# A one-layer hybrid decoder step: weight loads and stores moved from SP's DMA queue to POOL's, and a changed table of planned delays for TensorE's order

## Chip, core and metric

The kernel runs on one core of one Trainium2 chip. The metric is the device time of one execution in microseconds; lower is better. The time before is 1907.03 us, the median of three runs (1903.8, 1907.03 and 1909.56). The core has five engines that run their own instruction streams: PE (TensorE; its weight loads are listed as PEld), DVE (VectorE), ACT (ScalarE), POOL (GpSimd) and SP (SyncE, which here only issues DMAs).

## What is computed

One layer for a prompt of 1024 tokens and 8 samples of 8 tokens, 1088 columns in all, width 1024, float32:

```python
h = rmsnorm(x, norm_g)
p = jnp.einsum('btd,dc->btc', h, w_in)
q, k, v, ga, ps, gb, ma, mb = _split(p, IN_SIZES)
o = swa_banded(q, k, v, rel_bias, sinks_g)                # branch A, window 128
ya = jnp.einsum('btc,cd->btd', o * jax.nn.silu(ga), w_out_a)
yb_raw, wkv_T = rwkv_time_mix(ps, shift0, wkv0, ...)      # branch B, 16 heads of 64
yb = jnp.einsum('btc,cd->btd', yb_raw * jax.nn.silu(gb), w_out_b)
merged = jax.nn.sigmoid(ma) * ya + jax.nn.sigmoid(mb) * yb
out = x + jnp.einsum('btd,de->bte', merged, w_o)          # then a final rmsnorm
```

Inside `rwkv_time_mix` the projections r, k, v are mixed with those of the token before (z = ps + (prev - ps) * mu), decay and rate come from low-rank products, and a recurrence over the tokens updates one 64 x 64 state a head; its result is normalised by head and, with the term r*k*v added, multiplied by the gate. The outputs are y, the last keys and values, the states, and the last shift row.

## The kernel before

**Dense products.** All matrices are cut into 93 weight tiles of 1024 x 128. A float32 product is made of three float32r products: the weight is split in a high part `whi` (ACT, line 170) and a rest `wlo` (line 171), and the activations likewise in `hhi` and `hlo`. `load_w` (line 163) issues the load of a tile into the single buffer `wraw` and the two operations of the split. Each tile is multiplied with three chunks of columns (364, 364 and 360), 24 products a chunk, in two PSUM banks called d. The rest of the weight is computed on POOL in the recurrence's stage and on DVE in attention (`dve_lo`, line 276). A weight's buffers are double, so the rest of one tile waits until PE has finished the tile two before.

**Stages.** `start` normalises x. `rwkv` (line 484) runs the recurrence on 16 pieces s: four pairs of head groups times four quarters of 256 tokens. `attention` runs the window attention with the projections of its queries, and `final` the last projections. In `rwkv` one piece passes through these steps:

- front (lines 556 and 597, `quarter` once for each of two groups): loads zk, zr and zv of what `project` stored, the low-rank products (lo), the norm of the keys (kn), the product bo on the bonus term (line 686), the products A of the 64-token chunks, and two transposes t_k and t_v.
- invert (line 764): the 32 x 32 triangular blocks go to DRAM and come back in another layout (TM and TR), 31 steps of two operations follow on DVE (lines 784 and 786), and the result goes through DRAM again.
- merge (line 791): loads the inverse into `ti` (line 807) and joins the halves by the products q_a and q_b.
- chain (line 829): four chunks of 64 tokens in sequence. Each has three dependent products in bank c (lines 857, 864 and 869), with copies by ACT and DVE between them (xs and vsu), and ends with line 877, which adds the decayed state `sp` that POOL computed at line 853.
- posts (line 542): the products gc and gv of the head norm, three POOL operations (lines 945, 951 and 952), and the store to `d_y` (line 953). samples (line 532): the same recurrence for the samples, with products ss.

`project` (line 419) makes r, k and v: the evacuation in `shift_tile` writes two scaled copies by ACT (lines 403 and 404), POOL adds the shifted one (lines 405 and 412) into a buffer `zz`, of which there are two that other evacuations share, and line 424 stores it to `d_z`.

**What sets the order.** PE's order in these stages is written by a planner, `drive` (line 142). Each step is a generator that yields the delay after which its next product may stand, counted on the planner's clock, which advances with the products placed. A step that is ready is placed; otherwise four products of the dense stream are. The delays are the constants of lines 35 and 41: WI between the end of a front and the merge, WB between kn and bo, WM before q_a, WH and WS between the steps of a chain, WP between those of a post, WA, WD and WT elsewhere. HOLD is the time for which a single PSUM bank is kept free after its last use. The orders of ACT, DVE, POOL and SP are made by a scheduler from priorities. Each engine executes its list in order; so does SP's DMA queue, so that a DMA that waits holds up all that stand behind it.

Of the kernel before, what the change touches and what calls it, by code (L numbers as in the profile page):

```python
# [16 lines left out]
KT = 8  # L17
# [14 lines left out]
QORD = (4, 5, 6, 7) + tuple(range(NQS, 4)) + tuple(range(NQS))  # L32
FILL = (0, 0, 0, 0, 2, 2, 3, 2)
QD = 4
HOLD = 1.4
WV = 13.0
NYS = 6
MAN = {mybir.EngineType.PE, mybir.EngineType.SP, mybir.EngineType.Pool}
WX = 0.06
YPR = (200000, 0, 0)  # L40
WI, WD, WB, WA, WM, WH, WS, WP, WT = 34.0, 3.5, 9.0, 0.8, 4.0, 1.0, 1.7, 4.0, 10.0


T_LORA = 0
# [37 lines left out]
class Prog:  # L82
# [33 lines left out]
    def step(self, st):  # L116
# [7 lines left out]
        for tag in self.used:  # L124
            self.free[tag] = self.clk + HOLD
        self.used = set()
# [36 lines left out]
    def load_w(self, idx, pool=None, bufs=2, tag="", rpool=None, rbufs=1):  # L163
        nc = self.nc
        pool = pool or self.wp
        raw = (rpool or self.wp).tile([P, KT, P], F32, tag="wraw", name=f"wraw{idx}", bufs=rbufs)
        hi = pool.tile([P, KT, P], F32R, tag="whi" + tag, name=f"whi{idx}", bufs=bufs)
        lo = pool.tile([P, KT, P], F32R, tag="wlo" + tag, name=f"wlo{idx}", bufs=bufs)
        nc.sync.dma_start(raw, self.I["w"][idx].rearrange("p (k c) -> p k c", k=KT))
        nc.scalar.activation(hi, raw, AF.Copy)  # L170
        (nc.vector if self.dve_lo else nc.gpsimd).tensor_tensor(lo, raw, hi.bitcast(F32), ALU.subtract)  # L171
        return hi, lo
# [246 lines left out]
    def project(self, g):  # L419
        nc, ep = self.nc, self.ep  # L420
        base = T_RKVG + 4 * g
        for j in range(3):
            def out(c0, c1, z):
                nc.sync.dma_start(self.d_z[g][j][:, c0:c1], z[:, :c1 - c0])
                if j == 2:
                    self.mark(f"z{g}_{c0}")
            yield from self.shift_tile(base + j, 8 * j + g, out)
# [501 lines left out]
    def post(self, g, nm, t, w, y):  # L929
        nc, cp = self.nc, self.pp  # L930
        y = y[:, :w]
        rs = cp.tile([P, 320], F32, tag="gb", name=f"gn{nm}", bufs=2)[:, :w]
        parts = self.split(cp, y, w, f"c{nm}")
        yield None, WP, "t"
        ps = self.ps("t", f"gc{nm}")[:, :w]
        self.sum2(ps, self.cen, parts)
        nc.scalar.activation(rs, ps, AF.Square)
        nc.vector.tensor_copy(y, ps)
        parts = self.split(cp, rs, w, f"v{nm}")
        yield None, 1.0 + WP, "t"  # L940
        p2 = self.ps("t", f"gv{nm}")[:, :w]
        self.sum2(p2, self.bone, parts)
        nc.scalar.activation(rs, p2, AF.Ln, scale=1.0 / HD, bias=self.cst(C_EPS + 1, 1))
        nc.scalar.activation(rs, rs, AF.Exp, scale=-0.5)
        nc.gpsimd.tensor_tensor(y, y, rs, ALU.mult)
        nc.scalar.activation(y, y, AF.Identity, scale=self.par(Q_LG + g), bias=self.par(Q_LB + g))
        bt = cp.tile([P, 320], F32, tag="gb", name=f"bt{nm}", bufs=2)[:, :w]
        gt = cp.tile([P, 320], F32, tag="gb", name=f"gt{nm}", bufs=2)[:, :w]
        nc.sync.dma_start(bt, self.d_b[g][:, t:t + w])
        nc.sync.dma_start(gt, self.d_g[g][:, t:t + w])  # L950
        nc.gpsimd.tensor_tensor(y, y, bt, ALU.add)
        nc.gpsimd.tensor_tensor(y, y, gt, ALU.mult)
        nc.sync.dma_start(self.d_y[g][:, t:t + w], y)


    def attention(self, hs):
# [550 lines left out]
```

## Time and profile before

| | |
|---|---|
| median of three runs | 1907.03 us |
| the profiled execution's own time | 1908.33 us |
| its span, first to last instruction | 1906.5 us |
| PE busy | 1677.5 us (88%), mean granted clock 0.94 |
| DVE busy | 1193.9 us (63%) |
| ACT busy | 969.7 us (51%) |
| POOL busy | 414.6 us (22%), 490 instructions |
| moved by DMA | 209.33 MB, mean 110 GB/s |

Busy time is time in which an engine executes; a DMA's issue is not counted in it. The granted clock is the share of full speed that TensorE ran at. A wait is listed with the engine and line that waited, the one that released it, the total, the count and the longest.

### The profile page before, as it was taken

The page shows a single profiled execution, that of the slowest core. Times are in us where ns is not written, and L with a number is a line of the kernel's source. Part 1 is how long each engine was busy: PE and PEld are TensorE (multiplying, and loading weights), DVE is VectorE, ACT ScalarE, POOL GpSimd, SP SyncE. Part 2 cuts the span into 40 slices and gives each one's busy share as a digit, 9 for nine tenths or more (in the row PEclk, how much of TensorE's full clock was granted, in tenths as well). Part 3 has the DMA queues.
Part 4 walks back from the last instruction along what each step waited for, and adds up shares of the span by engine and source line. Part 5 has one row for each costly group of instructions (what it writes and reads, how often), then busy time and mean ns, then how long its engine had stood idle before and what let it go on. Part 6 is the DMA issues. An engine that isn't in the chain of part 4 may idle for free.

```text
span 1906.5 us, 33558 instructions
## 1 busy us (share of the span) xinstructions
PE 1677.5 (88%) x11744; PEld 1580.2 (83%) x11744; DVE 1193.9 (63%) x3563; ACT 969.7 (51%) x2494; POOL 414.6 (22%) x490
## 2 busy tenths in 40 slices
PE   5899697887787897786999887899999999999998
PEld 4899686776786887786889887889999889899997
DVE  6324868878768748669743778652266677544543
ACT  5346545654464545455545646644456765422232
POOL 4443223322422332123225112233100010000000
PEclk9999898988988988898999998999999999999999
DMA  4333423433333233332324333324422254374531
GB/s 161 134 97 113 108 85 86 120 92 96 107 84 102 79 101 113 103 86 88 99 72 138 113 105 98 93 75 138 146 91 65 75 167 131 103 247 139 174 110 58
DMA packets 217645, 209.33 MB, mean 110 GB/s; under 512 B 108452, under 2 KB 193044, under 8 KB 217444
## 3 DMA queue, kind: packets, MB, share of 16 engines
q1 hardware_dynamic: 216900, 204.22, 35.4%
q0 software_dynamic: 576, 2.96, 0.5%
q8 instruction: 93, 1.52, 0.3%
q14 instruction: 76, 0.62, 0.1%
HBM read 144.01 MB, written 65.07 MB: 110 GB/s over the span
## 4 chain that ended last, share of the span: by engine, by line
PE 58%; DVE 23%; ACT 6%; issue 5%; DMA 4%; POOL 2%; SPq 1%; DVEq 0%; POOLq 0%; ACTq 0%
PE d L110 37%; PE wo L110 5%; DVE TR L786 4%; DVE Tt L784 4%; PE c L110 3%; DVE KB L678 2%; PE s L110 2%; PE y L110 2%; PE o L110 2%; DVE vsu L877 1%; PE A L110 1%; PE pt L108 1%; POOL wlo L171 1%; DMA xt<-in_x 1%; DVE sg L650 1%
## 5 line engine op out<-in xcount | busy, mean ns | idle before, releaser
L110 PE MATMUL d<-hhi,whi 128*128 128x364 f32 (+1 forms) x1656 | 588.2, 355 | 52.9 <-ACT sho L414 23.0
L110 PE MATMUL d<-hlo,whi 128*128 128x364 f32 (+1 forms) x1656 | 567.1, 342 | 7.9 <-DVE hlo L350 6.9
L110 PEld LDWEIGHTS d<-hhi,whi 128*128 128x128 f32 x1656 | 331.1, 200 | 63.3 <-ACT sho L414 24.8
L110 PEld LDWEIGHTS d<-hlo,whi 128*128 128x128 f32 x1656 | 330.5, 200 | 13.3 <-DVE hlo L350 9.6
L110 PE MATMUL d<-hhi,wlo 128*128 128x364 f32 (+1 forms) x1656 | 336.9, 341 | 0.0
L110 PEld LDWEIGHTS d<-hhi,wlo 128*128 128x128 f32 x1656 | 285.5, 195 | 3.5 <-issue 3.3
L171 POOL TENSOR_TENSOR wlo<-wraw,whi 128x1024 fp32r<-128x1024 f32 x56 | 134.1, 2394 | 269.6 <-PE d L110 119.2
L786 DVE TENSOR_TENSOR TR<-TR,Tt 96x90 f32<-96x90 f32 (+26 forms) x496 | 142.7, 288 | 11.4
L784 DVE TENSOR_TENSOR Tt<-TM,TR 96x90 f32<-96x90 f32 (+26 forms) x496 | 138.8, 280 | 11.5
L170 ACT ACTIVATE whi<-wraw 128x1024 fp32r<-128x1024 f32 x90 | 95.0, 1056 | 73.0 <-PE d L110 52.7
L405 POOL TENSOR_TENSOR zz<-zz,pad 128x364 f32<-128x364 f32 (+1 forms) x75 | 74.1, 989 | 185.1 <-ACT zz L404 122.8
L853 POOL TENSOR_TENSOR sp<-vsu,pc 64x128 f32<-64x128 f32 x128 | 58.3, 455 | 222.4 <-DVE vsu L877 211.6
L877 DVE SCALAR_TENSOR_TENSOR vsu<-c,pc,sp 64x64 f32<-64x64 f32 x240 | 68.0, 283 | 18.9 <-PE c L110 14.3
L1080 ACT ACTIVATE sc<-sc,st 128x256 f32<-128x256 f32 (+1 forms) x128 | 61.8, 484 | 34.1 <-DVE st L1076 34.1
L403 ACT ACTIVATE pad<-d,prm 128x364 f32<-128x364 f32 (+1 forms) x75 | 40.7, 543 | 72.9 <-PE d L110 62.0
L1341 POOL TENSOR_TENSOR xr<-xr,frs 128x256 f32<-128x256 f32 x2 | 1.8, 934 | 341.5 <-ACT frs L1338 341.5
L678 DVE TENSOR_TENSOR KB<-e,sg 64x256 f32<-64x256 f32 x128 | 67.5, 537 | 1.2
L110 PE MATMUL d<-yhi,whi 128*128 128x364 f32 (+1 forms) x192 | 65.2, 340 | 0.0
L110 PE MATMUL d<-ylo,whi 128*128 128x364 f32 (+1 forms) x192 | 63.9, 333 | 0.0
L110 PE MATMUL d<-oh,whi 128*128 128x364 f32 (+1 forms) x192 | 63.2, 329 | 0.0
L110 PE MATMUL d<-ol,whi 128*128 128x364 f32 (+1 forms) x192 | 62.9, 328 | 0.0
L110 PE MATMUL wo<-ml,whi 128*128 128x416 f32 (+1 forms) x192 | 60.5, 329 | 0.0
(331 smaller groups left out, 3578.0 us busy)
## 6 DMA issues: line engine op xcount, KB each, us to landing
wraw<-in_w SPq DMA_DIRECT2D x93, 512.0 KB
d_z<-zz SPq DMA_DIRECT2D x48, 182.0 KB
zv<-d_z SPq DMA_DIRECT2D x48, 128.0 KB
d_m<-sp SPq DMA_DIRECT2D x32, 182.0 KB
TM<-s SPq DMA_DIRECT2D x72, 64.0 KB
stageo<-d_o SPq DMA_DIRECT2D x8, 544.0 KB
d_z<-zz SPq DMA_DIRECT2D x24, 180.0 KB
w<-in_lora SPq DMA_DIRECT2D x32, 128.0 KB
```

The lines of the kernel that those rows point to most:

```text
L108: self.nc.tensor.transpose(out, lhsT, rhs)
L110: self.nc.tensor.matmul(out, lhsT=lhsT, rhs=rhs, **kw)
L170: nc.scalar.activation(hi, raw, AF.Copy)
L171: (nc.vector if self.dve_lo else nc.gpsimd).tensor_tensor(lo, raw, hi.bitcast(F32), ALU.subtract)
L403: nc.scalar.activation(pad[:, 1:1 + m], ps[:, :m], AF.Copy, scale=mu)
L405: nc.gpsimd.tensor_tensor(z[:, :m], z[:, :m], pad[:, 0:m], ALU.add)
L678: nc.vector.tensor_tensor(KB[hr, :4, j, :], v64(t)[hr], d64(Pi, 1)[hr], ALU.mult)
L784: nc.vector.tensor_tensor(tv, M[s // 16][:np_, s % 16:s % 16 + 1, s + 1:32].to_broadcast([np_, cc, w]), R[:np_, 0:cc, s:s + 1].to_broadcas ...
L786: nc.vector.tensor_tensor(R[:np_, 0:cc, s + 1:32], R[:np_, 0:cc, s + 1:32], tv, ALU.add)
L853: nc.gpsimd.tensor_tensor(sp[h], vsu[h, c, :, h], pc[h, c].unsqueeze(2).to_broadcast([64, 2, HD]), ALU.mult)
L877: nc.vector.scalar_tensor_tensor(dst, pn[h, i, h], pc[h, c, i:i + 1], sp[h, i], ALU.mult, ALU.add)
L1080: nc.scalar.activation(sc[k], sc[k], AF.Exp, bias=st[:, 0, k:k + 1], accum_out=st[:, 1, k:k + 1])
```

## The change

The constants of the planner change, and three DMA statements name POOL's queue in place of SP's: the weight loads where POOL computes the rest (56 of the 90 that `load_w` issues; in attention and after they stay on SP), the 72 stores of z, and the 32 stores of y.

```diff
-HOLD = 1.4
+HOLD = 2.0
...
-WI, WD, WB, WA, WM, WH, WS, WP, WT = 34.0, 3.5, 9.0, 0.8, 4.0, 1.0, 1.7, 4.0, 10.0
+WI, WD, WB, WA, WM, WH, WS, WP, WT = 38.0, 3.5, 15.0, 0.8, 5.0, 1.4, 2.4, 5.0, 10.0
...
-        nc.sync.dma_start(raw, self.I["w"][idx].rearrange("p (k c) -> p k c", k=KT))
+        (nc.sync if self.dve_lo else nc.gpsimd).dma_start(raw, self.I["w"][idx].rearrange("p (k c) -> p k c", k=KT))
...
-                nc.sync.dma_start(self.d_z[g][j][:, c0:c1], z[:, :c1 - c0])
+                nc.gpsimd.dma_start(self.d_z[g][j][:, c0:c1], z[:, :c1 - c0])
...
-        nc.sync.dma_start(self.d_y[g][:, t:t + w], y)
+        nc.gpsimd.dma_start(self.d_y[g][:, t:t + w], y)
```

**PE, the first front's bo.** Before, the product bo0_0 of group 0, quarter 0 stands inside the third chunk of tile 5 (`d5_2`):

```order
L110 MATMUL d5_2_1197<-hhi728_153,whi5_956 128x360
L110 MATMUL d5_2_1197<-hlo728_154,whi5_956 128x360
L110 MATMUL bo0_0_1210<-shib0_0_1134,bone_171 128x256
L110 MATMUL bo0_0_1210<-slob0_0_1135,bone_171 128x256
L110 MATMUL A0_000_1227<-RA0_0_1125,KB0_0_1126 128x128
L110 MATMUL A0_001_1228<-RA0_0_1125,KB0_0_1126 128x128
```

Now it stands behind the whole first chunk of tile 6 (`d6_0`):

```order
L110 MATMUL d6_0_1240<-hhi0_143,whi6_1084 128x364
L110 MATMUL d6_0_1240<-hlo0_144,whi6_1084 128x364
L110 MATMUL d6_0_1240<-hhi0_143,wlo6_1085 128x364 x8
L110 MATMUL bo0_0_1272<-shib0_0_1134,bone_171 128x256
L110 MATMUL bo0_0_1272<-slob0_0_1135,bone_171 128x256
L110 MATMUL A0_000_1289<-RA0_0_1125,KB0_0_1126 128x128
L110 MATMUL A0_001_1290<-RA0_0_1125,KB0_0_1126 128x128
```

The last 12 products of d5_2 and the 24 of d6_0 have moved ahead of bo.

**PE, the third chunk of the last chain.** Before, products of a dense tile (`d37`) stand between the three steps of chunk c3_32 (the products y are its outputs):

```order
L110 MATMUL c3_32_14366<-vsu6_3_13244,am6_3_13246 128x128
L110 MATMUL c3_32_14366<-vsu6_3_13244,am7_3_13537 128x128
L110 MATMUL y3_32_14369<-r02_730,vsu6_3_13244 128x128
L110 MATMUL y3_32_14369<-r03_731,vsu6_3_13244 128x128
L110 MATMUL d37_0_14349<-hhi0_143,whi37_14085 128x364
L110 MATMUL d37_0_14349<-hlo0_144,whi37_14085 128x364
L110 MATMUL d37_0_14349<-hhi0_143,whi37_14085 128x364
L110 MATMUL d37_0_14349<-hlo0_144,whi37_14085 128x364
L110 MATMUL d37_0_14349<-hhi0_143,wlo37_14086 128x364 x4
L110 MATMUL c3_32_14366<-xs3_32_14367,ti_726 128x64 x2
L110 MATMUL d37_0_14349<-hhi0_143,wlo37_14086 128x364 x4
```

Now the steps follow each other, with no dense product between:

```order
L110 MATMUL c3_32_14916<-vsu6_3_13850,am6_3_13852 128x128
L110 MATMUL c3_32_14916<-vsu6_3_13850,am7_3_14255 128x128
L110 MATMUL y3_32_14919<-r02_730,vsu6_3_13850 128x128
L110 MATMUL y3_32_14919<-r03_731,vsu6_3_13850 128x128
L110 MATMUL c3_32_14916<-xs3_32_14917,ti_726 128x64 x2
L110 MATMUL c3_32_14916<-vsu6_3_13850,kbt6_3_13853 128x128
L110 MATMUL c3_32_14916<-vsu6_3_13850,kbt7_3_14256 128x128
L110 MATMUL y3_32_14919<-am6_3_13852,vsu6_3_13850 128x128
L110 MATMUL y3_32_14919<-am7_3_14255,vsu6_3_13850 128x128
```

The dense tiles that stood here and behind, down to tile 42, now stand earlier.

**SP and POOL, the merge of piece 9 (pair 2, quarter 1).** Before, SP's queue has weight loads (`wraw`) and stores of merge gates (`d_m`) around the store of the inverse (line 788) and its load into `ti` (line 807):

```order
L455 DMA d_m1_136<-sp56_0_8874 128x364
L1260 DMA mb1_0_17425<-d_m1_136 128x364
L455 DMA d_m1_136<-sp56_364_8928 128x364
L788 DMA s22_1_8539<-TR2_1_8542 352x1x32 x3
L169 DMA wraw27_9548<-in_w 128x1024
L455 DMA d_m1_136<-sp56_728_8981 128x360
L807 DMA ti_726<-s22_1_8539 32x8x32 x4
L779 DMA TR2_2_9373<-in_ri 96x352
```

Now at the same place:

```order
L589 DMA zk_5_3_10393<-d_z5_1_99 128x320
L788 DMA s22_1_9300<-TR2_1_9303 352x1x32 x3
L586 DMA w2_5_3_10389<-in_lora 128x256
L807 DMA ti_726<-s22_1_9300 32x8x32 x4
L950 DMA gt4_0_9854<-d_g4_111 128x256
L779 DMA TR2_2_10050<-in_ri 96x352
```

The load of tile 27, which stood between lines 788 and 807, has left the queue. On POOL it now follows the computation of the rest of tile 26, which frees the buffer, and each store of z (`d_z`) follows its addition:

```order
L853 TENSOR_TENSOR sp1_30_8419<-vsu2_3_7102,pc2_3_7103 64x128 x2
L171 TENSOR_TENSOR wlo26_7878<-wraw26_7876,whi26_7877 128x1024
L169 DMA wraw27_8069<-in_w 128x1024
L405 TENSOR_TENSOR zz6_0_7913<-zz6_0_7913,pad6_0_7912 128x364
L424 DMA d_z6_0_101<-zz6_0_7913 128x364
L405 TENSOR_TENSOR zz6_364_7954<-zz6_364_7954,pad6_364_7953 128x364
L424 DMA d_z6_0_101<-zz6_364_7954 128x364
L171 TENSOR_TENSOR wlo27_8071<-wraw27_8069,whi27_8070 128x1024
L945 TENSOR_TENSOR ysb1_20_7375<-ysb1_20_7375,gn2_2_7887 128x256
```

Nothing was taken off POOL for these rows; SP's list is shorter by 160 DMAs and POOL's longer by as many.

## The prediction

> **What bounds the kernel now.** I read the busy times by stage first, because one share over the whole span hides that this program has stages with different limits. Columns: stretch, its length, busy time of PE, PEld, DVE, ACT and POOL (with counts), granted TensorE clock, DMA share, GB/s.
>
> ```profile
> 61.30:177.50 116.20, 106.32 (x633) 104.55 (x634) 28.10 (x79) 51.85 (x126) 46.87 (x58) 0.96 0.38 127
> 177.50:1322.00 1144.50, 959.45 (x7057) 897.36 (x7056) 807.31 (x2522) 614.93 (x1647) 318.63 (x382) 0.91 0.34 98
> 1322.00:1665.00 343.00, 340.20 (x2510) 319.05 (x2510) 204.25 (x713) 198.00 (x543) 17.55 (x17) 0.99 0.36 114
> 1665.00:1906.50 241.50, 232.12 (x1392) 229.06 (x1388) 109.38 (x177) 69.20 (x104) 1.83 (x2) 0.99 0.45 145
> ```
>
> After 1322 us PE is idle for 2.8 us of 343 and 9.4 of 241.5, at a granted clock of 0.99: these stages are TensorE's own work and nothing in this change shortens them. The second row is the stage to watch, the RWKV recurrence with dense products between its steps: PE is idle 1144.5 - 959.45 = **185 us**, and its clock is 0.91, so that 959.45 x 0.09 = 86 us more go to slow products. The clock is low where PE pauses; stretches without pauses have 1.00:
>
> ```profile
> 1000.00:1050.00 50.00, 47.57 (x282) 45.89 (x281) 18.44 (x47) 27.69 (x70) 26.00 (x29) 1.00 0.45 139
> 1300.00:1350.00 50.00, 50.00 (x299) 48.76 (x298) 11.89 (x24) 22.41 (x44) 18.53 (x14) 1.00 0.56 174
> ```
>
> So one us of idle time costs about (185 + 86)/185 = 1.47 us here. These two rows show something else: PE full, DVE at 18 and 12 us of 50. There dense products run while the recurrence rests. Dense work is the cover for the recurrence's waits, and here it covers nothing.
>
> The second view is the list of waits of PE inside that stage (total us, times, longest):
>
> ```profile
> PE bo L110 <- ACT shib L235: 32.7, 9, 5.9
> PE c L110 <- DVE xs L861: 19.1, 14, 4.5
> PE d L110 <- ACT sho L414: 17.0, 3, 7.7
> PE t_10k L108 <- DVE zr L687: 14.0, 6, 4.2
> PE c L110 <- DVE vsu L866: 13.8, 17, 3.2
> PE d L110 <- ACT sp L220: 10.5, 5, 5.3
> PE q_3a L110 <- DVE ab L808: 8.6, 4, 3.9
> PE q_1a L110 <- DVE ab L808: 8.0, 6, 2.7
> PE q_0a L110 <- DVE ab L808: 7.3, 4, 2.9
> PE lo L110 <- ACT vsu L761: 6.7, 6, 2.2
> PE d L110 <- ACT zz L404: 6.2, 1, 6.2
> ...
> PE q_3a L110 <- DVE ysb L938: 3.9, 1, 3.9
> PE bo L110 <- DVE slob L236: 3.8, 6, 2.0
> PE q_2a L110 <- DVE ysb L938: 3.5, 1, 3.5
> PE c L110 <- DVE vsu L877: 3.5, 4, 1.4
> ```
>
> Three places hold most: bo, the second product of the front (36.5 us), q_a, the first of the merge (31.3), and the steps of the chain c (36.4). None of them names POOL or a DMA.
>
> **Part one, the planner's delays.** PE's order is fixed, so a longer planned delay means more dense products ahead of the waiting one. Counting dense products in the two orders: between kn and bo 42 on average before (24 to 56) and 71 now (52 to 92); between the last t_v of a front and q_a 154 and 189; inside one chain 83 and 101. The price of one comes from this row:
>
> ```profile
> 1322.27 58.33 PE d L110 x352
> ```
>
> 58.33/352 = 0.166 us. So bo gains 29 x 0.166 = 4.8 us of cover, q_a 5.8, a chain 3.0, which is 0.25 in each of its 12 steps. Against the longest waits, 5.9 at bo and 3.9 at q_a, that would clear nearly all of both; of the chain's waits (35, about 1.0 us each) a quarter, 9 us. HOLD, 0.6 longer, takes up to 0.6 from each of the six waits of t_10k and of lo: 6 us. First-order sum: 36 + 31 + 9 + 6 = **82 us**.
>
> I do not take all of it. The old cover was stretched by the very idle time and slow clock that go: the stage now runs 1144.5 - 271 = 873 us of full-speed work in 1144.5, a pace of 0.76, so 42 products lasted 42 x 0.166/0.76 = 9.2 us. With the 82 us and their clock gone the pace would be 873/(1144.5 - 120) = 0.85, and 71 products last 13.9 us: 4.7 longer than before, still below the 5.9 of the worst case; 154 and 189 products lasted 33.6 and would last 36.9, a gain of only 3.3 where the waits are up to 3.9. DVE, busy 807 us of 1144.5, has no fewer operations, and its queue becomes denser. So waits come back. Bounds: 0 (all come back) and 82; I take 22 at bo, 16 at q_a, 10 at c, t and lo together: **48 us**, near the upper row because the longest wait at bo is near the added cover.
>
> The dense products have to come from somewhere. Before, 3976 stand ahead of the recurrence's last product (gv of groups 6 and 7) and 344 follow it before the attention's second tile; now 4320 stand ahead and none follows. So 344 x 0.166 = 57 us move from behind the recurrence into it, and the last chain, which had 76 dense products, has **none**. What is bare there is priced from its last step:
>
> ```profile
> 1295.19 0.71 PE L110 MATMUL c<-vsu,am 128*128 128x128 f32 x4
> ...
> 1296.24 0.29 DVE L861 COPY xs<-c 64x128 f32<-64x128 f32 x1 [0.40 <-ACT xs L860]
> 1298.35 0.29 DVE L866 COPY vsu<-c 64x128 f32<-64x128 f32 x1 [1.81 <-ACT vsu L865]
> 1299.73 1.19 DVE L877 SCALAR_TENSOR_TENSOR so<-c,pc,sp 64x64 f32<-64x64 f32 x4 [1.09 <-PE c L110]
> ```
>
> From 1295.19 to 1300.92 is 5.7 us with PE full; I put 4.5 for a step with nothing between, an estimate, and four steps at 18, of which PE's own products and those of the samples fill about 12. That leaves 6; the merge ahead, the two posts behind, and the evacuations that must free a bank before the next tile starts I estimate at 3 each. New idle time **15 us**, between 5 (samples and posts fill more) and 25 (nothing overlaps).
>
> **Part two, 160 DMAs from SP's queue to POOL's**: 56 weight loads, 72 stores of z, 32 stores of y. SP's waits on POOL in the stage:
>
> ```profile
> SPq L169 <- POOL wlo L171: 95.0, 29, 6.9
> ...
> SPq L424 <- POOL zz L405: 61.6, 24, 6.4
> SPq L953 <- POOL ysb L952: 40.3, 25, 3.5
> ```
>
> These 197 us of a blocked queue go, since on POOL the DMA stands behind its own producer. What it buys is what stood behind them and was ready. One stall on PE shows the blockage from end to end:
>
> ```profile
> 217.73 0.31 POOL L412 TENSOR_TENSOR zz<-zz,pad 128x64 f32<-128x64 f32 x1
> ...
> 234.72 0.85 SPq L424 DMA_DIRECT2D d_z<-zz  x2
> ...
> 237.71 1.05 ACT L404 ACTIVATE zz<-d,prd 128x364 f32<-128x364 f32 x2 [3.84 <-DMA d_z<-zz]
> 238.33 0.67 PE L110 MATMUL d<-hhi,whi 128*128 128x360 f32 x1 [6.19 <-ACT zz L404]
> ```
>
> z is finished at 218.04, its store leaves SP 16.7 us later, ACT waits for the buffer, PE for ACT. On POOL the store follows the addition: this **6 us** goes. The other late evacuations (sho 17.0, sp 10.5) follow ACT and other stores, which stay on SP: 0, at best half, 14.
>
> The cost is POOL's time.
>
> ```profile
> L169 SPq DMA_DIRECT2D wraw<-in_w x90: 327/333/1155, 71.9 to 1813.7; - x90
> L385 POOL DMA_DIRECT2D out_ck<-in_ckn x1: 605/605/605, 80.2 to 80.2; - x1
> ```
>
> An issue takes 0.33 us on SP and 0.6 on POOL, so POOL gets 160 x 0.6 = 96 us more beside its 319 of 1144.5. I count nothing, because POOL is idle 70% of the stage and its result for the chain, sp, is wanted only at the end of a step (4.5 us above). Without that cover each of 64 chunks would pay up to 0.6: 38 us. Where wlo waits for a tile's last product on PE, stores and loads behind it on POOL wait too; before, the weight loads did so on SP.
>
> The Trainium skill, "DMA: Bandwidth & Descriptors", section "Issuing engines are not separate DMA queues", says that DMAs from any engine share the same 16 DMA engines and that issuing from several saves only the issue time, usually small. By that rule part two is worth nothing and the sum below loses its 6 us and their clock; the stall at 238 us speaks against it, since a queue's order cost 16.7 us there.
>
> **Sum**, against the profiled execution's own 1908.33 us (span 1906.5; the median of the three runs shown is 1907.03): -(48 + 6) x 1.47 + 15 x 1.47 = -79 + 22 = -57. From the median: **1850 us**. A difference below about 0.3%, 6 us, can't be told from none here.
>
> **The rivals.** (1) The whole first-order relief: -(82 + 6 - 15) x 1.47 = -107, **1800**; with half of sho and sp too, 1779. For it: the waits are short and many, and SP's relief shortens the loads between front and merge. Against it: the pace above. (2) **Slower.** The chain and front take as long as their own engines need, the waits move along with the longer plan, and only the bare tail remains: +22 to +37, **1929 to 1944**. It decides once less than 15 us of the 185 are saved. For it: DVE at 71% of the stage, and waits that name DVE's or ACT's latest result, so that more cover helps only as far as their queues allow. Against it: the 344 products that now lie in a stage with 185 us of idle PE. (3) POOL becomes late: descriptors wait for DVE. Its sum: if each of the 56 weight tiles were late by an issue and a DVE copy, 0.6 + 0.29, that is 50 us, **1900**. For it: loads now stand behind POOL's other work in order; against it: POOL's idle 70%, and no wait of PE on wlo above. The Trainium skill, "SBUF — State Buffer", section "SBUF: two separate sides", says that while DVE runs a copy in its two-port mode POOL cannot write the descriptors of DMAs issued from its queue; no run here shows that yet. (4) The queues change nothing and the plan works: -(48 - 15) x 1.47 = -49, 1858, inside the forecast.
>
> **How the numbers follow.** Forecast with (4), 1815 to 1890: 0.52. Rival 1: 0.16. Rival 3, 1890 to 1912: 0.14, half of it within 0.3%. Rival 2: 0.18, a third of it mild and below 1920. Faster than 1901: 0.52 + 0.16 + 0.07 = 0.75; within 0.3%: 0.08; slower: 0.17. The range, 1785 to 1920, leaves out about 0.05 below and 0.12 above.
>
> **What would show it.** Right: in the changed profile PE waits of bo and q_a at half or less, a granted clock of 0.94 or more in the stage, no full stretch of PE with an idle DVE near 1000 and 1310 us, no store of z late by over 5 us; a PE gap of some 15 us shared among the last chain's steps. Wrong: bo and q_a with their old totals while the stage holds 57 us more products (rival 2), or PE or ACT waiting for POOL or a weight load (rival 3).

## The result, and the profile after

The changed kernel takes **1861.96 us** (median of 4 runs, 1860.32 to 1868.65), the kernel before 1907.4 (median of 4, 1903.8 to 1909.56): a ratio of 0.977, 95% interval 0.9742 to 0.9798, 45 us saved where 57 were forecast. The profiled execution is the slowest of the four, 1868.65 us with a span of 1866.9.

The first view is again the busy times by stretch of the changed kernel (stretch, length, busy time of PE, PEld, DVE, ACT, POOL, granted clock, DMA share, GB/s). The recurrence now ends at 1331, its last gv.

```profile
177.50:1333.80 1156.30, 1001.09 (x7414) 943.81 (x7412) 837.91 (x2540) 631.69 (x1683) 394.29 (x520) 0.93 0.36 102
1000.00:1050.00 50.00, 41.31 (x329) 39.51 (x329) 32.04 (x97) 27.92 (x75) 11.96 (x14) 0.90 0.37 102
1300.00:1350.00 50.00, 35.95 (x192) 31.47 (x192) 25.29 (x50) 20.12 (x46) 14.82 (x20) 0.76 0.45 129
242.00:1283.50 1041.50, 909.94 (x6799) 860.41 (x6799) 774.11 (x2359) 586.69 (x1562) 356.11 (x473) 0.94 0.37 104
1283.50:1331.00 47.50, 35.81 (x277) 30.12 (x277) 20.05 (x52) 12.10 (x36) 9.49 (x15) 0.82 0.19 58
```

In all, PE idles 1156.3 - 1001.09 = 155 us of the recurrence's stage, where it was 185. The two 50 us rows answer those of the prediction: at 1000 us the stretch of full PE beside an idle DVE is gone, and at 1300 us it has turned into the opposite, PE at 36 of 50 and a clock of 0.76. The last row is the tail from the last merge on: 47.5 - 35.81 = 11.7 us idle.

The waits of PE in that stage, to 1334 us (total us, times, longest; `...` stands for rows left out):

```profile
PE c L110 <- DVE xs L861: 22.3, 15, 4.0
PE d L110 <- ACT zz L404: 18.2, 6, 4.5
PE d L110 <- DVE gz L435: 17.0, 4, 8.8
PE c L110 <- DVE vsu L866: 15.7, 18, 2.6
PE t_00k L108 <- DVE zr L687: 9.6, 3, 4.2
PE t_10k L108 <- DVE zr L687: 5.9, 1, 5.9
...
PE d L110 <- ACT sp L220: 4.9, 4, 2.0
...
PE d L110 <- ACT sho L414: 4.6, 3, 2.8
...
PE q_0a L110 <- DVE ab L808: 3.0, 2, 1.5
PE d L110 <- DVE qs L1069: 2.8, 1, 2.8
...
PE c L110 <- DVE vsu L877: 1.8, 4, 0.6
PE q_3a L110 <- DVE ab L808: 1.6, 1, 1.6
PE q_1a L110 <- DVE ab L808: 1.2, 2, 0.7
```

bo, at 36.5 us the largest, is no longer in the list; q_a has 5.8 of 31.3 left. The chain's three rows sum to 39.8 and are no shorter than before (36.4). Products of a dense tile, d, wait for evacuations that must free a bank. They did so before, but in other places: behind sho and sp (L220) these waits fell from 27.5 us to 9.5, behind ACT's zz and DVE's gz they rose from 9.6 (6.2 and 3.4) to 35.2.

On the moved DMAs, POOL's timeline of the changed kernel at one z store (start, us, engine, line, operation, wait ahead):

```profile
221.78 0.96 POOL L405 TENSOR_TENSOR zz<-zz,pad 128x364 f32<-128x364 f32 x1 [9.89 <-ACT zz L404]
223.04 0.56 POOL L424 DMA_DIRECT2D d_z<-zz  x1 [0.30 <-DVE pad L409]
```

and what SP waits for now (SPq):

```profile
SPq L950 <- POOL ysb L945: 72.2, 24, 8.5
SPq L688 <- DVE TR L786: 66.9, 9, 18.3
SPq L586 <- DVE w2l L591: 63.9, 16, 9.6
...
SPq L624 <- DMA d_b<-zr: 50.2, 27, 4.0
```

The store leaves 0.3 us behind its addition, where one had left 16.7 us late. But SP is as blocked as ever: all rows of its waits add up to 763 us before and 823 now. L950 waits as it did (74.0 us before), and L688, L586 and L624, whose rows were 16.1, 14.4 and 13.6, stand in the place of L169, L424 and L953. Taking three instructions out of an in-order queue let others wait in their stead.

### The profile page after: what moved, and what is told of

Same layout as the page of the kernel before. It is cut to its first block, busy times and chain, and to the rows that moved or that the text cites. A ratio compares the mean times of both kernels' runs of the same rounds, so it can differ in the third digit from the quotient of the medians.

```text
span 1866.9 us, 33535 instructions
## 1 busy us (share of the span) xinstructions
PE 1662.3 (89%) x11744; PEld 1568.0 (84%) x11744; DVE 1213.3 (65%) x3563; ACT 965.9 (52%) x2494; POOL 498.9 (27%) x650
## 4 chain that ended last, share of the span: by engine, by line
PE 53%; DVE 25%; ACT 6%; DMA 6%; issue 5%; POOL 3%; SPq 1%; DVEq 0%; POOLq 0%; ACTq 0%
PE d L110 32%; DVE TR L786 6%; PE wo L110 5%; DVE Tt L784 5%; PE c L110 3%; DVE KB L678 2%; PE s L110 2%; PE o L110 2%; DVE vsu L877 2%; PE pt L108 1%; PE y L110 1%; PE A L110 1%; DMA TM<-s 1%; POOL wlo L171 1%; DMA wraw<-in_w 1%
## 5 line engine op out<-in xcount | busy, mean ns | idle before, releaser
L110 PE MATMUL d<-hhi,wlo 128*128 128x364 f32 (+1 forms) x1656 | 333.0, 339 | 0.0
L786 DVE TENSOR_TENSOR TR<-TR,Tt 96x90 f32<-96x90 f32 (+26 forms) x496 | 149.5, 302 | 11.9
L110 PEld LDWEIGHTS c<-xs,ti 128*128 128x128 f32 x256 | 38.4, 205 | 30.8 <-DVE xs L861 28.4
```

The costliest lines, as they stand in the source:

```text
L110: self.nc.tensor.matmul(out, lhsT=lhsT, rhs=rhs, **kw)
L786: nc.vector.tensor_tensor(R[:np_, 0:cc, s + 1:32], R[:np_, 0:cc, s + 1:32], tv, ALU.add)
```

## The experiments

The question was which part earns the 45 us. All ratios are against the kernel before on the same chip, with 95% intervals.

**The two halves apart.** The plan alone is the changed kernel with

```diff
-(nc.sync if self.dve_lo else nc.gpsimd).dma_start(raw, ...)
+nc.sync.dma_start(raw, ...)
-nc.gpsimd.dma_start(self.d_z[g][j][:, c0:c1], ...)
+nc.sync.dma_start(self.d_z[g][j][:, c0:c1], ...)
-nc.gpsimd.dma_start(self.d_y[g][:, t:t + w], y)
+nc.sync.dma_start(self.d_y[g][:, t:t + w], y)
```

> The new delays with all 160 DMAs back on SP's queue. Theory A (the plan carries the gain, as in the sum of the prediction: 33 us of idle time x 1.47 from the plan, 9 us from the queues): 1865 to 1875 us, with bo and q_a gone from PE's waits as in the changed kernel and a z store that leaves SP over 5 us late again. Theory B (the longer plan needs the relieved SP queue, because loads between front and merge would otherwise be late): 1885 us or more, with PE or DVE waiting for DMAs. The rule that issuing from several queues saves only issue time gives the time of the changed kernel, 1860 to 1864.

Measured: 1851.65 us (1842.86 to 1857.56), ratio 0.971 (0.9669 to 0.9751). It is below every time expected, and 10 us under the changed kernel's median. Stores of z are late again, by up to 9 us, and yet no product waits over 4.0 us for zz (the row is shown below): the stall of 6.2 us that the prediction laid to a late store is gone with the plan alone. The queues alone, with the old numbers:

```diff
-HOLD = 2.0
+HOLD = 1.4
-WI, WD, WB, WA, WM, WH, WS, WP, WT = 38.0, 3.5, 15.0, 0.8, 5.0, 1.4, 2.4, 5.0, 10.0
+WI, WD, WB, WA, WM, WH, WS, WP, WT = 34.0, 3.5, 9.0, 0.8, 4.0, 1.0, 1.7, 4.0, 10.0
```

> The old delays with the 160 DMAs on POOL's queue. Theory A: about 6 us of idle time goes with its share of the clock, 9 us, so 1895 to 1902. Theory C (the queues are what the change is worth): 1880 or less, with the waits of bo and q_a shorter although the number of dense products between them is that of before. If POOL's issues of about 0.58 us hurt: over 1910, with DVE or PE waiting for POOL.

Measured: 1919.54 us (1917.92 to 1919.74), ratio 1.0068 (1.0041 to 1.0095): **13 us slower**, where theory A had 5 to 12 us of gain. The time is that of the last expectation, over 1910, but of its sign little is there: no wait of PE names POOL, DVE's waits that do add up to 20.5 us where they were 16.2, and ACT's to 30.2 where they were 22.0. The stall behind the late store did go (d<-zz 6.2 to 1.6 us), while d<-sho rose from 17.0 to 22.5. All the gain is the plan's, and the queue change takes back some of it. With the new plan the two ratios, 0.977 and 0.971, differ by 0.006 with half-widths of 0.003 and 0.004: a loss of about 10 us there too, of which the sign is barely sure and the size is not.

**Only the loads, or only the stores, on POOL**, with the new plan: of the first diff above only the last two pairs of lines (loads stay on POOL), then only the first pair (stores stay on POOL).

> The new delays, only the 56 weight loads on POOL's queue; the 104 stores of z and y on SP. Theory A: the stall behind a late z store is there again, 5 to 10 us over the changed kernel, 1867 to 1873. If loads are what blocked SP (95.0 us of its waits on POOL before, of 197): as the changed kernel, 1860 to 1865.

> The new delays, only the 72 stores of z and the 32 of y on POOL's queue; the weight loads on SP. Theory A: as the changed kernel within 4 us, 1858 to 1866, since the one stall that the queues relieve hangs on a z store. If the weight loads matter: 1870 or more, with z stores on time but other stores on SP late behind a weight load that waits for POOL.

Measured: loads 1855.44 us, ratio 0.9735 (0.9701 to 0.9769); stores 1854.09, ratio 0.9725 (0.9688 to 0.9762). Both lie below every time expected, and between the plan alone and both moves, but both intervals hold the plan's 0.971. The two can't be told apart. Neither shows the relief of a z store: d<-zz waits least where nothing is moved. The rows are those of the plan alone, the loads moved and the stores moved; with both moved it was 18.2 us.

```profile
PE d L110 <- ACT zz L404: 15.0, 6, 4.0
PE d L110 <- ACT zz L404: 19.6, 7, 4.1
PE d L110 <- ACT zz L404: 16.8, 6, 4.0
```

**Is it POOL's time?** Three kernels keep before's plan and all DMAs on SP, and give POOL one more instruction at each of the 160 places. The first adds 176 elements of a tile of its own:

```diff
+self.junk_op()    # gpsimd.tensor_tensor(junk[:, :176], junk[:, 176:], junk[:, 176:], ALU.add)
 nc.sync.dma_start(...)
```

> The kernel before, all DMAs on SP, with one more POOL instruction of about 0.57 us (an addition on a tile of its own) at each of the 160 places, so POOL has the time of the issues but not the DMAs. The other engines' orders are nearly those of before (41 differing lines on DVE, where the queue change alone makes 699). Theory P (the queue change costs time because POOL is late by its issues): 1913 to 1922, as the run with the queues alone. Theory O (it costs time because DVE's and ACT's instructions are placed in another order once the DMAs stand elsewhere, or by the path of the DMAs): 1902 to 1910, as before.

Measured: 1951.84 us, ratio 1.0243 (1.0205 to 1.028), which neither theory gave. Its row from 61 to 177 us, the stretch ahead of the recurrence's, tells why:

```profile
61.30:177.50 116.20, 71.90 (x372) 69.46 (x372) 18.04 (x38) 29.00 (x68) 99.70 (x188) 0.80 0.24 82
```

POOL has 188 instructions there instead of 58. The additions wait for nothing, so 130 of them were put there, and PE is busy 34 us less than before (106.32). The run says nothing of the question. The second reads the producer's result, so that it can't run ahead:

```diff
+self.junk_op(z[:, :160], z[:, 120:280])    # gpsimd.tensor_tensor(junk, a, b, ALU.add)
 nc.sync.dma_start(self.d_z[g][j][:, c0:c1], ...)
```

> The kernel before, all DMAs on SP, with an addition of 0.5 to 0.6 us on POOL behind each of the 160 producers, reading its result (so it can't run ahead of it) and writing a tile of its own. DVE's order differs from that of before in 38 lines, the queue change's in 699. Theory P (POOL's time for the issues is the cost of the queue change): 1914 to 1923 us, as with the queues alone. Theory O (the new order on DVE and ACT, or the DMAs' own path, is the cost): 1902 to 1911, as before.

Measured: 1922.84 us, ratio 1.009 (1.0057 to 1.0124), as theory P has it. But its trace mixes two effects. Here are the stretches from the first to the last merge. Before:

```profile
227.00:1268.10 1041.10, 864.51 (x6355) 807.35 (x6354) 747.40 (x2345) 559.62 (x1507) 285.16 (x352) 0.90 0.34 98
```

This run, with the additions:

```profile
231.10:1282.30 1051.20, 864.50 (x6357) 807.12 (x6356) 763.23 (x2345) 559.77 (x1507) 350.69 (x468) 0.91 0.34 97
```

The queues alone:

```profile
226.30:1277.80 1051.50, 877.55 (x6355) 818.81 (x6354) 746.16 (x2344) 559.03 (x1506) 352.77 (x467) 0.89 0.33 96
```

And the next run, with small DMAs:

```profile
225.60:1272.80 1047.20, 867.42 (x6355) 810.31 (x6354) 754.78 (x2345) 560.63 (x1507) 350.61 (x468) 0.90 0.34 98
```

The same 2345 DVE instructions (2344 in one trace) take 763 us beside the additions and 747 without; beside the issues of the queues alone they take 746. So the additions bring a cost on DVE that this trace of the queues alone doesn't have, and their 1922.84 us can't be put down to POOL's time alone. Whether issues too slow DVE isn't settled: with the small DMAs DVE takes 755 us, and under the new plan 774 us with the queue change (2359 instructions, above) and 766 without (2358, below). The third kernel, for the issues without the additions, has POOL issue 160 small DMAs, with the real ones still on SP:

```diff
+nc.gpsimd.dma_start(d_junk[k], z[:, :16])
 nc.sync.dma_start(self.d_z[g][j][:, c0:c1], ...)
```

> The kernel before, its 160 DMAs still on SP, with one small DMA (128x16, to scratch of its own) issued by POOL behind each of the 160 producers: POOL has the issues of the change, SP has its old queue, and DVE's order differs from that of before in 20 lines. Theory P (the issues themselves, about 0.57 us each on POOL, are the cost): 1914 to 1922, as with the queues alone, with DVE's busy time per instruction unchanged. Theory Q (the issues are free, and the queue change costs by the new order on DVE or by stores and loads that stand behind POOL's other work; the loss of the run with additions on POOL came from DVE, whose 2345 instructions between the first and the last merge took 763 us there and 747 before): 1902 to 1911.

Measured: 1913.91 us (10 runs), ratio 1.0034 (1.0015 to 1.0054), between the two theories: 160 issues on POOL, with their small transfers, cost 3 to 10 us, against 8 to 18 of the whole move. The rest, if there is one, may lie in the order on DVE, which the move changes in 699 lines and this run in 20, or in where loads and stores stand on POOL. That stays open: no run kept POOL's queue and DVE's old order together. Nor does one trace settle it. In the profiled execution of the queues alone PE idles no more than before (174.0 us and 176.6), and its products take 13 us longer at a clock of 0.89; its other three runs had mean clocks of 0.940 to 0.942 (0.932 in the profiled one) and the same time.

**The plan by its parts**, each alone on the kernel before:

```diff
-WB 9.0
+WB 15.0                                     # bo_sp
-WI 34.0, WM 4.0
+WI 38.0, WM 5.0                             # merge_sp
-HOLD 1.4, WH 1.0, WS 1.7, WP 4.0
+HOLD 2.0, WH 1.4, WS 2.4, WP 5.0            # steps_sp
```

> The kernel before with WB alone at 15.0; all DMAs on SP. Dense products between kn and bo 42 -> 68, between t_v and q_a 154 -> 166; the last chain keeps 80 of them, so no bare tail. Theory A (the terms of the prediction's sum add up): the bo term alone, 22 us of idle time x 1.47 = 32, so about 1875 us. Theory B (waits move along, a part alone brings little and only all delays together free the stage): 1895 us or more, with the time that leaves bo appearing at q_a or c.

> The kernel before with WI 38.0 and WM 5.0 alone. Dense products between t_v and q_a 154 -> 177, bo and the chains as before, 76 left for the last chain. Theory A: the q_a term alone, 16 us x 1.47 = 24, so about 1883 us. Theory B: 1898 or more, since q_a is late with DVE's solution of the front, which gets no faster.

> The kernel before with HOLD 2.0, WH 1.4, WS 2.4 and WP 5.0 alone. Dense products inside a chain 84 -> 108, bo as before. The prediction gave these 10 us of idle time, 15 us of time: 1892. But the changed kernel's list shows c waiting 39.8 us where it was 36.4 before, so theory A now says that this part gives nothing: 1900 to 1912, with c's three waits not under 33 us. If 1892 or less, the longer steps pay elsewhere (t, lo, ss).

Measured: WB alone 1878.38 us, ratio 0.9858 (0.982 to 0.9896), 29 us saved; WI and WM 1874.83, 0.9848 (0.9804 to 0.9892), 33 us; the steps **1856.39, 0.9744 (0.9703 to 0.9784), 51 us**, which its interval can't tell from the whole plan's 0.971. The three sum to 114 us, and together they give 55. The stage to the last gv, for WB alone, for WI and WM, for the steps, and for the whole plan on SP (to the first product behind it):

```profile
177.50:1301.90 1124.40, 951.56 (x7124) 890.61 (x7123) 823.24 (x2528) 612.35 (x1652) 324.71 (x382) 0.93 0.36 101
177.50:1291.70 1114.20, 953.32 (x7109) 887.14 (x7108) 817.15 (x2522) 613.26 (x1648) 318.43 (x383) 0.94 0.36 102
177.50:1286.90 1109.40, 955.77 (x7172) 900.45 (x7171) 819.42 (x2524) 617.43 (x1655) 315.34 (x383) 0.93 0.36 103
177.50:1314.50 1137.00, 994.30 (x7419) 937.39 (x7417) 829.30 (x2541) 631.13 (x1685) 321.59 (x389) 0.94 0.36 104
```

PE's idle time, 185 us before, is 173, 161, 154 and 143: 12, 24, 31 and 42 us saved. So WB met the time that theory A gave it, 1875, but half by theory B's mechanism. bo's wait is gone; the chains, which now hold 78 dense products instead of 84, wait 45.5 us where it was 36.4, and d<-gz 23.3 where it was 3.4:

```profile
PE c L110 <- DVE vsu L866: 26.9, 20, 4.3
PE d L110 <- DVE gz L435: 23.3, 4, 9.2
PE c L110 <- DVE xs L861: 15.3, 16, 2.9
```

The waits with the steps alone:

```profile
PE c L110 <- DVE xs L861: 17.5, 12, 3.0
PE bo L110 <- ACT shib L235: 17.0, 7, 4.8
...
PE c L110 <- DVE vsu L866: 5.4, 8, 2.8
...
PE bo L110 <- DVE slob L236: 4.5, 6, 2.3
...
PE c L110 <- DVE vsu L877: 2.7, 3, 1.2
```

With its own delays alone the chain waits 25.6 us and no longer 36.4, and bo, at an unchanged 42 dense products, 21.5 and no longer 36.5. In the full plan the same delays leave c at 39.8. Why bo gains isn't shown: this part also has HOLD, and WH stands as well between q_a and the products behind it and between the steps of the samples; no run took these apart. The expectation that the steps give nothing, read off that row, was wrong: a row of the full plan doesn't tell what one of its parts does alone.

**A covered tail.** Two kernels with all DMAs on SP leave 104 dense products for the last chain, where the full plan leaves none:

```diff
-WI 38.0, WB 15.0, WM 5.0
+WI 36.0, WB 12.0, WM 5.0                    # plan_middle
+WI 34.0, WB 15.0, WM 4.0                    # bo_steps_sp
```

> All DMAs on SP, new HOLD, WM, WH, WS, WP, but WI 36.0 and WB 12.0, between old and new. Dense products: bo 57 (71 with the full plan), q_a 177 (189), chains 109 (102), and 104 are left for the last chain (0 with the full plan). If the bare tail is worth its 13.7 us of idle time and the shorter covers cost little: 20 us less than the full plan on SP, less what bo and q_a take back (14 and 12 products each time, 2 us at 32 and 16 places, of which the full plan's lists show nearly no wait): 1830 to 1845. If the covers of bo and q_a are needed in full: 1850 to 1860, the idle time only moved from the tail to bo.

> All DMAs on SP, all new numbers but WI 34.0 and WM 4.0 as before. Dense products: bo 70, q_a 166, chains 106, and 104 stay for the last chain. If a covered tail is worth its 13.7 us of idle time and q_a's shorter cover costs less than that (q_a waited 27 us in the run with the steps alone, at 165 products): 1835 to 1850, better than the full plan on SP. If the idle time only moves, as it did with WI 36.0 and WB 12.0: 1852 to 1866.

Measured: 1865.12 us, ratio 0.9785 (0.9756 to 0.9814), and 1859.22, ratio 0.9749 (0.9709 to 0.9788). The first is above both of its expectations, the second inside the one by which idle time only moves. Neither beats the full plan on SP; the second can't be told from it. The full plan on SP, up to the last merge and in the tail:

```profile
241.00:1263.80 1022.80, 901.30 (x6795) 852.49 (x6795) 766.20 (x2358) 584.05 (x1559) 291.08 (x357) 0.95 0.37 105
1263.80:1311.70 47.90, 37.47 (x280) 31.39 (x280) 19.90 (x52) 12.07 (x36) 8.48 (x13) 0.79 0.21 66
```

The first of the two, likewise:

```profile
231.20:1278.20 1047.00, 895.87 (x6631) 843.13 (x6632) 769.57 (x2351) 573.54 (x1546) 289.55 (x356) 0.93 0.35 101
1278.20:1329.50 51.30, 50.12 (x425) 46.85 (x425) 23.12 (x57) 21.28 (x54) 8.90 (x12) 1.00 0.29 94
```

The tail's idle time falls from 10.4 us to 1.2 as meant, but up to the last merge it rises from 121.5 to 151.1. In this run covering the tail costs more than the tail.

The plan alone, all DMAs on SP, has the lowest time measured, 1851.65 us; the full change, the steps alone and several others have intervals that overlap with its own.

## Why the prediction was right, step by step

The time came out 12 us above the forecast and well inside its range. That it came so near is in part luck, since two errors of opposite sign lie behind it: the plan alone gave 55 us where the sum has 49, and the queues took 10 to 13 where the sum has them give 9.

- **The plan, forecast -(48 - 15) x 1.47 = -49 us: right, measured -55.** In the changed kernel's own trace the stage up to the last merge lost idle time from 185 - 0.3, the old tail's part, to 155.2 - 11.7 - 2.8 = 140.7 us (2.8 is the wait d<-qs behind the last gv). That is 44 saved where the prediction put 48 + 6. In the trace of the plan alone the whole stage, bare tail included, lost 42 us where the sum has 48 - 15 = 33.
- **The bare tail, 15 us: right.** 11.7 + 2.8 = 14.5 us; the clock in the 50 us row from 1300 is 0.76. Inside it the chain's steps waited 3.0 us, not 6, and the samples, which were to fill them, waited 4.1 themselves.
- **1.47 us of time for one of idle time: right here, but not a constant.** 30 us less idle time in the stage x 1.47 = 44; the medians differ by 45 and the profiled executions by 40. In the plan alone's trace 42 us of idle time and 60 of time are saved, a factor of 1.4. But WB alone saved 12 us of idle time and 28 of time in its trace, and the queues alone took 11 us more with no more idle time, since the products took longer. The clock rose from 0.91 to 0.93, a little under the 0.94 named.
- **bo and q_a, 22 and 16 us: the places were right, the sizes not.** Their waits lost 36.5 and 25.5 us. The runs with one part give 29 and 33 us of time, against 22 and 16 x 1.47 = 32 and 24, and 12 and 24 us of idle time against 22 and 16. So bo's agreement in time is luck. "Waits come back" was right as well, but they came back elsewhere: d<-zz and d<-gz in the full plan, c and d<-gz with WB alone.
- **c, t and lo together, 10 us: wrong in both views.** In the full plan these waits didn't fall (c 36.4 to 39.8; t_10k fell from 14.0 to 5.9, but t_00k is new with 9.6). Alone the delays saved 31 us of idle time and 51 of time. The term is mis-sized because it prices 3.0 us of cover per chain against c's own waits. Alone these lost 10.8 us, close to the 9 counted, and bo lost 15 at an unchanged count, which the sum gave to WB only. That longer steps leave ACT and DVE time between the chain's demands is a possible reason, not a shown one.
- **Part two, "this 6 us goes", with POOL's 96 us of issues of which it says "I count nothing": wrong in sign.** The stall did go, but it goes with the plan alone too, and the forecast of -9 us is +13 measured alone. Idle 70% of a stage is no proof that an engine's time is free: 160 issues on POOL, with their small transfers, cost 3 to 10 us. The forecast's own figure without cover, 38 us, was the bound that should have kept a share of the sum. What it left out altogether is that DVE's and ACT's order is drawn up anew when a DMA changes its engine; whether that costs time isn't shown.

The rivals: full relief (1800) fell, because c, t and lo gave nothing in the full plan and waits came back at the dense tiles' evacuations. The slower one, where waits move along and only the tail remains, fell on bo and q_a. POOL late (1900) was right in that the move costs time, 13 us alone rather than 50, but its named cause, descriptors that wait for DVE, doesn't show in the issues (below). "The queues change nothing", 1858, came nearest to the time, though the queues do change something.

The Trainium skill, "DMA: Bandwidth & Descriptors", section "Issuing engines are not separate DMA queues", has the DMA engines shared and only the issue time saved by issuing elsewhere. The runs agree that nothing is gained: 1919.54 us with the queues alone and 1851.65 without the move. They add that the issue time saved on one engine is spent on the other, and that it is more there: 0.33 us on SP, and on POOL

```profile
L424 POOL DMA_DIRECT2D d_z<-zz x72: 542/563/634, 86.5 to 915.3; - x72
L169 POOL DMA_DIRECT2D wraw<-in_w x56: 541/577/624, 67.5 to 1224.6; - x56
```

These rows (least, median and longest, in ns) also bear on the descriptors that wait for DVE, the rule of the Trainium skill, "SBUF — State Buffer", section "SBUF: two separate sides", weighed in rival 3: no issue of the 128 took over 634 ns, with DVE busy 72% of the stage, so the 0.29 us of a DVE copy that the rival adds to each isn't there. From issue to landing a store of z took 2.4 us (median; at most 5.6) and a load 4.0 (at most 6.4); what made the latest ones late no run shows.

## What to carry to other kernels

A blocked in-order queue is worth relieving only if what stands next in it is ready: here 197 us of SP's waits went and others took their place. Price a DMA that is moved by the time it takes on its new engine, and look at what the move does to the order on engines that it doesn't touch. Where several delays feed from one supply of cover, measure each alone, since their gains overlap (114 us summed, 55 together), and one part may hold nearly all of it.

## What the runs showed of the hardware that was not expected

A DVE instruction can be held up for as long as POOL executes. The rows are from the timeline of the run with the queues alone. DVE:

```profile
668.62 0.22 DVE L784 TENSOR_TENSOR Tt<-TM,TR 120x54 f32<-120x54 f32 x1
668.75 0.15 DVE L402 COPY pad<-pad 128x1 f32<-128x1 f32 x1
668.87 3.51 DVE L786 TENSOR_TENSOR TR<-TR,Tt 120x54 f32<-120x54 f32 x1
672.41 0.22 DVE L784 TENSOR_TENSOR Tt<-TM,TR 120x45 f32<-120x45 f32 x1
```

POOL at the same time:

```profile
669.13 2.40 POOL L171 TENSOR_TENSOR wlo<-wraw,whi 128x1024 fp32r<-128x1024 f32 x1
671.47 0.82 POOL L405 TENSOR_TENSOR zz<-zz,pad 128x296 f32<-128x296 f32 x1
```

A DVE instruction whose neighbours take 0.22 us took 3.51, and ended at 672.38, beside the end of POOL's second instruction (672.29). The Trainium skill, "SBUF — State Buffer", section "SBUF: two separate sides", says that a DVE instruction with two SBUF inputs and a POOL instruction that reads SBUF exclude one another for a whole instruction; the trace agrees that one waits for the other whole. Which of the two began first can't be read here: by these rows DVE did, by 0.26 us, and was held all the same. With each DVE instruction that the timelines list by itself held against the median of its line and shape, the excess of those over 0.15 us too long adds up to 99 us in the stage before and 110 in the changed kernel, over half of it in instructions that overlap wlo (58 and 59); all of them overlap a POOL instruction. DVE is late in bursts, and this adds to them. One of the new waits of the changed kernel is behind such a burst: the busy times of that stretch,

```profile
321.50:338.30 16.80, 7.09 (x47) 6.31 (x45) 16.26 (x52) 8.19 (x20) 6.49 (x8) 0.87 0.25 76
```

two of its instructions on DVE,

```profile
330.06 2.27 DVE L786 TENSOR_TENSOR TR<-TR,Tt 96x75 f32<-96x75 f32 x1
337.73 0.54 DVE L435 TENSOR_TENSOR gz<-d,gz 128x364 f32<-128x364 f32 x1
```

and PE:

```profile
338.32 0.67 PE L110 MATMUL d<-hhi,whi 128*128 128x364 f32 x1 [8.78 <-DVE gz L435]
```

DVE is busy 16.26 of 16.8 us, 2.27 of them in one stretched instruction beside wlo, and gz, for which PE waits 8.78 us, stands in that queue. No run moved wlo from POOL, so what that would be worth was not tried.
